# A hybrid attention layer on one core: z of the softmax heads made before v, gate sigmoids moved, half of P divided by ScalarE

## The chip, the cores and the metric

The kernel runs on one core of one Trainium2 chip. The time is device microseconds (us) of one launch. Engines: PE (TensorE), PEld (its weight loads), DVE (VectorE), ACT (ScalarE), POOL (GpSimd) and SP (SyncE, which here only issues DMAs). Each engine works through its own queue in order.

## The reference, cut to what matters

x is 512 x 1024, one batch, one layer; eight softmax heads (branch a) and eight stick-breaking heads (branch b), each 64 wide.

```python
h = rms_norm(x, norm_w)
qa, ka, va, za, qb, kb, vb, zb, gl_a, gl_b = split(h @ w_in)     # 8 x 512, 2 x 1024
oa = moba_attention(rms_norm(qa), rms_norm(ka), va, rel_bias)    # softmax(q k / 8 + bias[t - s]), s <= t
ob = stick_breaking_attention(qb, kb, vb)                        # A[t,s] = b_ts * prod_{s<j<t}(1 - b_tj)
ya = (oa * silu(za)) @ w_up_moba
yb = (ob * silu(zb)) @ w_up_sb
y  = sigmoid(gl_a + gb[:1024]) * ya + sigmoid(gl_b + gb[1024:]) * yb
return x + y @ w_out
```

## The kernel before

**Products in three parts.** Every fp32 operand is split into a high and a low half in fp32r, and each product is three matmuls (mm3, L233 high by low, L234 low by high, L235 high by high). For a weight block the low half is therefore read by the second matmul of its chunk.

**Weights.** They come as blocks of 128 x 1024 (512 KB, `wr`), loaded by SP (L159) in a fixed order, split by ACT into `wh` (L187) and by DVE into `wl` (L189). Each of the three has 3 buffers, so wl of block n+3 can be made only when block n has been used up. The number in a tile's name (wl55) is the block's place in that order. A chunk of one block is 24 matmuls over 512 columns.

**Stages.** First qa and ka with their row norms; then the seven chunks of FRONT while the norms and the transposed q and k are made; then v (values, blocks of sums and differences in seven products X, Y, Z) and q of branch b; then eight pairs of heads, a0 to a3 and b0 to b3; at the end the up products of b and the output projection.

**A pair of heads.** PE makes the scores of two heads (L512), then the weighted sum with v of the pair two before (weighted, L604; its result `po` is multiplied by z at L609 and split at L750 and L751). Per head of a, softmax() (L526) loads the bias, adds it and takes the row's extreme (DVE L532), takes Exp with the row sum (ACT L534), the reciprocal (DVE L535) and divides the rows (DVE L537). Rows come as four tiles, tile 3 with 512 columns to tile 0 with 128. Per head of b, stick() (L542) takes two sigmoids of each tile (ACT L550, L551, L560, L561), a scan of running products (DVE L554, L564) and a multiply (DVE L556, L566). Then P is transposed in 32 x 32 blocks (turn, DVE L576), written to memory by four SP DMAs (put, L583) and read back by a DMA of ACT's queue (get, L590).

**The fills.** Between these steps PE gets chunks from the table FILLS, four entries a pair: one behind P of each head, and two after that. The words are za and zb (f_z: sigmoid of the chunk on ACT L617, multiplied by it on DVE L618, both read the PSUM bank), k and q (split(), ACT L420 and DVE L421), g (f_g: a gate chunk, evicted by one ACT Sigmoid with the bias, L631), and up (the up product of a, multiplied into the gates at L769). Chunks that stand in the front use the six PSUM banks of tag "s"; in the pairs those of tag "pj", which has two.

**What sets the order.** The list scheduler of the framework puts the instructions of each engine into its queue by data dependences and its own estimates; `issue_after` adds a dependence where the code wants one (in stick(), for example, the first sigmoid of a pair comes after the last weight split, and the sigmoids of the second head after the last gate eviction in `evicted`). Exp and Sigmoid lie in different tables of ACT, so each change between them has an ACT_TABLE_LOAD in the queue.

Of the kernel before, what the change touches and what calls it, by code (L numbers as in the profile page):

```python
# [12 lines left out]
AF = mybir.ActivationFunctionType  # L13
ALU = mybir.AluOpType
# [28 lines left out]
Y_SUMS = {0: ("T2b",), 2: ("T3a", "T3b"), 5: ("T4a", "T4b")}  # L43


FRONT = ("g:0", "g:1", "g:2", "g:3", "g:4", "g:5", "g:6")
FILLS = ("za:0", "k:0 q:0", "", "",
         "za:1", "g:7 q:1", "k:1", "",
         "za:2", "g:8", "zb:0", "",
         "za:3", "k:2 q:2", "g:9", "",  # L50
         "zb:1", "g:10", "k:3 q:3", "",
         "zb:2", "g:11", "up:0", "",
         "zb:3", "g:12", "up:1", "",
         "g:13", "g:14", "up:2", "up:3",
         "g:15")


@with_exitstack
def hybrid_layer(ctx: ExitStack, tc: tile.TileContext, x, xT, w, rel, out):
    nc = tc.nc  # L60
    V, A, G, T = nc.vector, nc.scalar, nc.gpsimd, nc.tensor
# [16 lines left out]
    def slot(name, dt=F32):  # L78
        return gp.tile([P, S], dt, tag="g", name=name)
# [15 lines left out]
    nw, mb, qw, kw = sm[:, 0:8], sm[:, 8:24], sm[:, 24:25], sm[:, 25:26]  # L95
# [8 lines left out]
    VOUT, QOUT = ([(kind, b + h) for b in ORDER[kind] for h in HALVES[kind]] for kind in "vq")  # L104
    stream = list(range(8)) + list(range(20, 20 + len(FRONT))) + VOUT + QOUT + list(range(20 + len(FRONT), WO)) + OUT

# [24 lines left out]
    def each(step, kind, names, after):  # L131

        for name in names:
            for half in HALVES[kind]:
                after = step(kind, name, half, after)
        return after
# [224 lines left out]
    def mix_x(k):  # L361

        a, b = xraw[k], xraw[k + 4]
        left, right = slice(0, HS), slice(HS, S)
        V.tensor_tensor(b[:, right], a[:, right], b[:, right], op=ALU.subtract)
        V.tensor_tensor(a[:, right], a[:, left], a[:, right], op=ALU.subtract)
        V.tensor_tensor(a[:, left], b[:, right], a[:, left], op=ALU.subtract)
        V.tensor_tensor(b[:, left], b[:, left], a[:, left], op=ALU.add)
        h = tp.tile([P, 4 * PQ], F32R, tag="pt", bufs=4, name=f"mx{k}")
        if k < 2:  # L370
            l = tp.tile([P, 4 * PQ], F32R, tag="turned", bufs=2, name=f"ml{k}")
            l = [l[:, n * S:(n + 1) * S] for n in range(2)]
        else:
            l = [tp.tile([P, S], F32R, tag=("p3", "sx")[n], bufs=2, name=f"ml{k}{n}") for n in range(2)]
        for n, raw in enumerate((a, b)):
            hi, lo = h[:, n * S:(n + 1) * S], l[n]
            A.activation(hi, raw, AF.Copy)
            V.tensor_tensor(lo, raw, hi.bitcast(F32), op=ALU.subtract)
            for cs, name in ((left, ("S2", "S4")[n]), (right, ("S3", "S1")[n])):
                mixed[name, k] = hi[:, cs], lo[:, cs]  # L380
# [68 lines left out]
    def split_flipped(raws, name):  # L449

        res = []
        for p, raw in enumerate(raws):
            hi, lo = slot(f"{name}{p}h", F32R), slot(f"{name}{p}l", F32R)
            src = raw.rearrange("p (a i r) -> p i a r", a=4, i=NT)
            h, l = (by_block(blocks(x)) for x in (hi, lo))
            if name == "qa":
                whole = slot(f"{name}{p}")
                A.activation(by_block(mirror(whole)), src, AF.Copy, scale=nqk)
                src, h, l = whole, hi, lo
            A.activation(h, src, AF.Copy)  # L460
            V.tensor_tensor(l, src, h.bitcast(F32), op=ALU.subtract)
            res.append((hi, lo))
        return res
# [5 lines left out]
    def norm(ps, name, **order):  # L469
        st[name] = head_norm(ps, name, **order)  # L470

    def spread(ps, name):
        with tc.issue_after(low[count[0] - 2]):
            rows = head_rows(ps, name, st[name])
        flipped[name] = flip(rows, name)
# [3 lines left out]
    def bring(name):  # L479
        raws[name] = fetch(flipped[name], name)  # L480
# [11 lines left out]
    def chunk_ct(name):  # L492
        hi, lo = load_w()
        ps = bank(home[0], name)
        for k in range(KT):
            ks = slice(k * P, (k + 1) * P)
            mm3(ps, hi[:, ks], lo[:, ks], xH[k], xL[k], k == 0, k == KT - 1)
        return ps
# [20 lines left out]
    def row_tiles(br, h):  # L519

        p10 = tp.tile([P, 3 * P], F32, tag="p1", bufs=2, name=f"p{br}{h}1")
        return {3: tp.tile([P, S], F32, tag="p3", bufs=2, name=f"p{br}{h}3"),
                2: tp.tile([P, 3 * P], F32, tag="p2", bufs=2, name=f"p{br}{h}2"),
                1: p10[:, :2 * P], 0: p10[:, 2 * P:], (1, 0): p10}

    def softmax(h, sc, bias):  # L526
        rows = row_tiles("a", h)
        m = tp.tile([P, 3, NT], F32, tag="m", bufs=4, name=f"m{h}")
        for two in ((3, 2), (1, 0)):
            for i in two:  # L530
                n = (i + 1) * P
                V.tensor_tensor_reduce(rows[i], sc[i], bias[:, S - n:], scale=1.0, scalar=3e38, op0=ALU.add,  # L532
                                       op1=ALU.min, accum_out=m[:, 0, i:i + 1])
                A.activation(rows[i], rows[i], AF.Exp, bias=m[:, 0, i:i + 1], scale=-1.0, accum_out=m[:, 1, i:i + 1])  # L534
            V.reciprocal(m[:, 2, two[1]:two[0] + 1], m[:, 1, two[1]:two[0] + 1])  # L535
            for i in two:
                V.tensor_scalar(rows[i], rows[i], m[:, 2, i:i + 1], None, op0=ALU.mult)  # L537
        return rows

    evicted = []  # L540
# [73 lines left out]
    def f_z(br, p):  # L614
        ps = chunk_ct(f"z{br}{p}")
        zr[br, p] = slot(f"z{br}{p}")
        A.activation(zr[br, p], ps, AF.Sigmoid)  # L617
        V.tensor_tensor(zr[br, p], ps, zr[br, p], op=ALU.mult)  # L618
# [7 lines left out]
    gates = {}  # L626

    def f_g(i):
        ps = chunk_ct(f"gl{i}")
        g = slot(f"gl{i}")  # L630
        evicted.append(A.activation(g, ps, AF.Sigmoid, bias=mb[:, i:i + 1]).ins)  # L631
        gates[i] = g

    for i, word in enumerate(FRONT):
        f_g(int(word.split(":")[1]))
        if i == 0:
            norm(ps_ka, "ka", after=summed[0])
            mix_x(0)
        elif i == 1:
            mix_x(1)  # L640
            summed.append(each(add_sum, "v", ("T3",), last["ka"]))
        elif i == 2:
            bring("qa")
            mix_x(2)
        elif i == 3:
            spread(ps_ka, "ka")
            mix_x(3)
        elif i == 4:
            bring("ka")
        elif i == 5:  # L650
            qa.extend(split_flipped(raws["qa"], "qa"))
# [152 lines left out]
    def split_3(k):  # L804
# [2 lines left out]
        part(*s3[k], gates[k], slice(0, HS))  # L807


    make = {"za": lambda i: f_z("a", i), "zb": lambda i: f_z("b", i), "q": f_q, "k": f_k, "g": f_g,  # L810
            "up": lambda i: up("a", i)}
    fills = [[(kind, int(i)) for kind, i in (word.split(":") for word in part.split())] for part in FILLS]

    def fill(tag="pj"):

        for kind, i in fills.pop(0):
            home[0] = "s" if kind == "up" else tag
            make[kind](i)
# [7 lines left out]
    def finish(m, tag="s"):  # L826

        br, p = PAIRS[m]
        weighted(tag, br, p, v_of[br], [done.pop((m, b)) for b in range(2)])
        split_o(br, p)  # L830

    early[0] = True
    for m, (br, p) in enumerate(PAIRS):
        q, k = (qa, ka) if br == "a" else (qb, kb)
        sc = {h: {} for h in (2 * p, 2 * p + 1)}
        with tc.issue_after(end[0]):
            scores(br, p, q, k, sc)
        if m > 1:
            finish(m - 2, "pj")
        for b in range(2):  # L840
            h = 2 * p + b
            bias = load_bias(h) if br == "a" else None
            done[m, b] = put(br, h, turn(br, h, (softmax if br == "a" else stick)(h, sc[h], bias)))
            fill()
            if not b:
                done[m, 0] = get(*head(m, 0), done[m, 0])
        for b in range(2):
            if not b:
                done[m, 1] = get(*head(m, 1), done[m, 1])
            if (m, b) in SUMS:  # L850
                sum_w(SUMS[m, b], done[m, b])
            fill("pj" if (b or not fills[1]) and m < 7 else "s")
# [77 lines left out]
    for c in range(2):  # L930
        hi, lo = load_w()
        for t, ps, a, b in parts:
            for kk in range(2):
                k = 2 * c + kk
# [20 lines left out]
def _layout(x, norm_w, w_in, merge_gate_b, q_norm_w, k_norm_w, rel_bias, w_up_moba, w_up_sb, w_out):  # L955
# [24 lines left out]
    first = {"za": 1536, "g": 4096, "k": 2560, "zb": 3584}  # L980
    for kind, i in (word.split(":") for word in " ".join(FRONT + FILLS).split()):
        if kind == "up":
# [32 lines left out]
```

## Time and profile before

| what | value |
|---|---|
| median of three runs (lowest, highest) | 384.65 us (384.2, 386.11) |
| profiled execution | 384.15 us |
| span of its instructions | 382.4 us |
| mean granted clock of PE | 0.999 |
| HBM read and written | 67.65 MB and 14.70 MB |

The profile is one execution. A row of a group shows its busy time, the mean of one in ns, and the idle time before it with what ended it. A row of the timeline begins with its start and its length in us; matmul lengths overlap, so their rate is read from their starts. L numbers are lines of the kernel before; those of the kernel after are up to 12 higher.

### The profile page before, as it was taken

What the parts mean: (1) busy time and instruction counts of PE and PEld (TensorE: products, weight loads), DVE (VectorE), ACT (ScalarE), POOL (GpSimd) and SP (SyncE); (2) the same over time, 40 slices, a digit from 0 to 9 for tenths busy, and PEclk for the clock granted to TensorE, in tenths of its full rate; (3) what the DMA queues carried; (4) which work ended last, traced back from release to release, by engine and by line L of the source; (5) the groups of instructions that cost most, each with busy time, mean ns of one, the idle gap of its engine ahead of it and who ended that gap; (6) DMA issues with size and microseconds to landing.
All of it is one profiled execution on the core that took longest, in us unless ns stands there. A gap on an engine that the chain in (4) does not pass through costs nothing.

```text
span 382.4 us, 5493 instructions
## 1 busy us (share of the span) xinstructions
PE 377.9 (99%) x1935; PEld 308.8 (81%) x1935; DVE 290.9 (76%) x503; ACT 211.3 (55%) x353; POOL 78.5 (21%) x124
## 2 busy tenths in 40 slices
PE   8999999999999999999999999999999999999996
PEld 5888888888888998887887878787878877888885
DVE  4828998934786468993889689798988825999962
ACT  5675657346754537772886773553554322368540
POOL 3859959220210200000000000010000000420310
PEclk9999999999999999999999999999999999999999
DMA  7989898996673755869767765869788881599964
GB/s 271 340 328 340 212 198 301 252 326 245 152 197 92 204 128 183 210 207 285 244 162 236 224 235 154 285 165 312 248 242 285 207 301 56 157 264 292 163 164 172
DMA packets 36747, 86.38 MB, mean 226 GB/s; under 512 B 3944, under 2 KB 16744, under 8 KB 36720
## 3 DMA queue, kind: packets, MB, share of 16 engines
q1 hardware_dynamic: 27696, 52.72, 41.2%
q0 software_dynamic: 6576, 22.57, 25.0%
q10 hardware_dynamic: 2448, 10.75, 8.5%
q8 instruction: 15, 0.25, 0.3%
q14 instruction: 12, 0.10, 0.1%
HBM read 67.65 MB, written 14.70 MB: 215 GB/s over the span
## 4 chain that ended last, share of the span: by engine, by line
PE 99%; DVE 0%; issue 0%
PE gl L233 8%; PE gl L234 8%; PE gl L235 8%; PE poa L604 2%; PE pob L604 2%; PE sb L512 2%; PE sa L512 2%; PE za L233 2%; PE zb L233 2%; PE yb L233 2%; PE za L234 2%; PE zb L234 2%; PE yb L234 2%; PE ka L234 2%; PE ka L233 2%; PE kb L234 2%
## 5 line engine op out<-in xcount | busy, mean ns | idle before, releaser
L189 DVE TENSOR_TENSOR wl<-wr,wh 128x1024 fp32r<-128x1024 f32 (+1 forms) x61 | 71.8, 1181 | 31.6 <-ACT wh L187 31.5
L187 ACT ACTIVATE wh<-wr 128x1024 fp32r<-128x1024 f32 (+1 forms) x61 | 62.8, 1029 | 41.0 <-DMA wr<-in_w 9.6
L233 PE MATMUL gl<-xl,wh 128*128 128x512 f32 x128 | 50.0, 390 | 0.0
L234 PE MATMUL gl<-xh,wl 128*128 128x512 f32 x128 | 49.9, 390 | 0.0
L235 PE MATMUL gl<-xh,wh 128*128 128x512 f32 x128 | 49.8, 389 | 0.0
L140 POOL COPY turn_of<-ptb 1x1 f32<-1x1 f32 x3 | 0.7, 245 | 147.9 <-DMA ptb<-pdb 147.9
L233 PEld LDWEIGHTS gl<-xl,wh 128*128 128x128 f32 x128 | 24.0, 188 | 5.3 <-issue 0.2
L235 PEld LDWEIGHTS gl<-xh,wh 128*128 128x128 f32 x128 | 24.0, 188 | 5.0
L234 PEld LDWEIGHTS gl<-xh,wl 128*128 128x128 f32 x128 | 24.0, 188 | 4.9
L631 ACT ACTIVATE gl<-gl,x 128x512 f32<-128x512 f32 x16 | 11.0, 686 | 23.1 <-PE gl L235 22.7
L554 DVE TENSOR_TENSOR_SCAN sx<-om,begin 128x512 f32<-128x512 f32 (+1 forms) x16 | 17.0, 1078 | 4.5 <-ACT om L550 4.5
L534 ACT ACTIVATE pa<-pa,m 128x512 f32<-128x512 f32 (+3 forms) x32 | 17.6, 552 | 1.4 <-DVE m L532 1.3
L576 DVE STREAM_TRANSPOSE turnedb<-pb 128x384 f32<-128x384 f32 (+1 forms) x24 | 14.0, 602 | 0.1
L532 DVE CUSTOM_DVE_ANT_0 pa<-sa,om 128x512 f32<-128x512 f32 (+3 forms) x32 | 13.9, 485 | 0.0
L576 DVE STREAM_TRANSPOSE turneda<-pa 128x384 f32<-128x384 f32 (+1 forms) x24 | 13.7, 602 | 0.0
L233 PE MATMUL za<-xl,wh 128*128 128x512 f32 x32 | 12.9, 404 | 0.0
L233 PE MATMUL zb<-xl,wh 128*128 128x512 f32 x32 | 12.8, 400 | 0.0
L233 PE MATMUL yb<-olb,wh 128*128 128x512 f32 x32 | 12.6, 393 | 0.0
L234 PE MATMUL za<-xh,wl 128*128 128x512 f32 x32 | 12.5, 390 | 0.0
L234 PE MATMUL zb<-xh,wl 128*128 128x512 f32 x32 | 12.5, 390 | 0.0
L234 PE MATMUL yb<-ohb,wl 128*128 128x512 f32 x32 | 12.5, 390 | 0.0
L234 PE MATMUL ka<-wh,xl 128*128 128x512 f32 x32 | 12.5, 390 | 0.0
(428 smaller groups left out, 1070.6 us busy)
## 6 DMA issues: line engine op xcount, KB each, us to landing
wr<-in_w SPq DMA_DIRECT2D x57, 512.0 KB, 5.6
pda<-turneda SPq DMA_DIRECT2D x32, 160.0 KB, 2.9
pta<-pda ACTq DMA_DIRECT2D x8, 640.0 KB, 4.5
pdb<-turnedb SPq DMA_DIRECT2D x32, 160.0 KB, 4.2
ptb<-pdb ACTq DMA_DIRECT2D x8, 640.0 KB, 6.3
qT<-in_w POOLq DMA_DIRECT2D x6, 512.0 KB, 6.3
xn<-in_x SPq DMA_DIRECT2D x8, 256.0 KB, 6.5
om<-e_dr SPq DMA_DIRECT2D x8, 256.0 KB, 4.1
```

The lines of the kernel that those rows point to most:

```text
L187: high[c] = A.activation(hi[:, a:b], raw[:, a:b], AF.Copy).ins
L189: low[c] = V.tensor_tensor(lo[:, a:b], raw[:, a:b], hi[:, a:b].bitcast(F32), op=ALU.subtract).ins
L233: T.matmul(ps, aH, bL, start=start, stop=False, skip_group_check=on)
L234: T.matmul(ps, aL, bH, start=False, stop=False, skip_group_check=on)
L235: end[0] = T.matmul(ps, aH, bH, start=False, stop=stop, skip_group_check=on).ins
L512: T.matmul(ps[b][:, c:c + n], x[o, i * P:(i + 1) * P], y[o, :n], start=m == 0, stop=m == 2)
L532: V.tensor_tensor_reduce(rows[i], sc[i], bias[:, S - n:], scale=1.0, scalar=3e38, op0=ALU.add, op1=ALU.min, accum_out=m[:, 0, i:i + 1])
L534: A.activation(rows[i], rows[i], AF.Exp, bias=m[:, 0, i:i + 1], scale=-1.0, accum_out=m[:, 1, i:i + 1])
L554: V.tensor_tensor_scan(sx[:, n - 1::-1] if n == S else sx[:, :n][:, ::-1], om[:, S + 1 - n:][:, ::-1], begin[:, S - n:S][:, ::-1], 0.0, op ...
L576: V.transpose(turned[:, :, at:at + n, :].rearrange("p q j r -> p j q r"), rows[i].rearrange("p (j q c) -> p j q c", j=n, q=4))
L604: guard[0] = T.matmul(po[o, :].rearrange("p (a n r) -> p a n r", a=4, r=32)[:, :, i:i + n, :], vv[j][:, c:c + HD], src, start=j == NT - 1, ...
L631: evicted.append(A.activation(g, ps, AF.Sigmoid, bias=mb[:, i:i + 1]).ins)
```

## The change

It has four parts. FRONT holds three gates and the four z chunks of branch a in place of seven gates. FILLS is written anew: gates g:3 to g:10 stand beside the softmax pairs, z of b beside its own pairs, in each pair's first entry. A gate chunk made in a softmax pair is evicted with Identity plus bias and gets its Sigmoid later, in place, from a new word "s" in the entries of pairs b0, b1 and b2, behind the newest gate eviction. In softmax() the divides of tiles 3 and 2 go from DVE to ACT (Copy with a scale per row); tiles 1 and 0 stay.

```diff
-FRONT = ("g:0", "g:1", "g:2", "g:3", "g:4", "g:5", "g:6")
+FRONT = ("g:0", "g:1", "g:2", "za:0", "za:1", "za:2", "za:3")
...
-         "za:3", "k:2 q:2", "g:9", "",
-         "zb:1", "g:10", "k:3 q:3", "",
+         "k:2 q:2", "g:9", "g:10", "",
+         "zb:0", "g:11", "k:3 q:3 s:3 s:4", "",
...
             for i in two:
-                V.tensor_scalar(rows[i], rows[i], m[:, 2, i:i + 1], None, op0=ALU.mult)
+                if i > 1:
+                    A.activation(rows[i], rows[i], AF.Copy, scale=m[:, 2, i:i + 1])
+                else:
+                    V.tensor_scalar(rows[i], rows[i], m[:, 2, i:i + 1], None, op0=ALU.mult)
...
-        evicted.append(A.activation(g, ps, AF.Sigmoid, bias=mb[:, i:i + 1]).ins)
+        evicted.append(A.activation(g, ps, AF.Identity if raw[0] else AF.Sigmoid, bias=mb[:, i:i + 1]).ins)
...
+    raw = [False]
+
+    def f_s(i):
+        with tc.issue_after(evicted[-1]):
+            A.activation(gates[i], gates[i], AF.Sigmoid)
+
     for i, word in enumerate(FRONT):
-        f_g(int(word.split(":")[1]))
+        kind, n = word.split(":")
+        f_g(int(n)) if kind == "g" else f_z("a", int(n))
...
     for m, (br, p) in enumerate(PAIRS):
+        raw[0] = br == "a"
```

The table moves instructions on all engines. Three places follow; the number behind an underscore only tells tiles of one name apart.

**Place 1, ACT's queue at the end of pair a3, before.** `pa7` are the rows of head 7 with their Exp, `m7` its row numbers, `pta6` the read of head 6's transposed rows, `wh48` a weight split, `om1` the first sigmoid of pair b0.

```order
L534 ACTIVATE pa73_2164,m7_2166<-pa73_2164,m7_2166 128x512
L534 ACTIVATE pa72_2165,m7_2166<-pa72_2165,m7_2166 128x384
L534 ACTIVATE pa71_2163,m7_2166<-pa71_2163,m7_2166 128x256
L534 ACTIVATE pa71_2163,m7_2166<-pa71_2163,m7_2166 128x128
L187 ACTIVATE wh47_2190<-wr47_2130 128x1024
L420 ACTIVATE kb2h_2221<-kb2_2196 128x512
L590 DMA pta6_2160<-pda6_2121 128x1280
L420 ACTIVATE qb2h_2225<-qb1_1260 128x512
L187 ACTIVATE wh48_2231<-wr48_2194 128x1024
L631 ACT_TABLE_LOAD
L631 ACTIVATE gl9_2262<-gl9_2237,x0_78 128x512
L550 ACTIVATE om1_121<-sb03_2264 128x512
```

The same place in the changed kernel:

```order
L594 DMA pta6_2165<-pda6_2121 128x1280
L188 ACTIVATE wh47_2195<-wr47_2130 128x1024
L635 ACTIVATE gl10_2261<-gl10_2236,x0_78 128x512
L535 ACTIVATE pa73_2169,m7_2171<-pa73_2169,m7_2171 128x512
L535 ACTIVATE pa72_2170,m7_2171<-pa72_2170,m7_2171 128x384
L535 ACTIVATE pa71_2168,m7_2171<-pa71_2168,m7_2171 128x256
L535 ACTIVATE pa71_2168,m7_2171<-pa71_2168,m7_2171 128x128
L539 ACTIVATE pa73_2169<-pa73_2169,m7_2171 128x512
L539 ACTIVATE pa72_2170<-pa72_2170,m7_2171 128x384
L188 ACTIVATE wh48_2230<-wr48_2199 128x1024
L554 ACT_TABLE_LOAD
L554 ACTIVATE om1_121<-sb03_2263 128x512
```

The eviction of the pair's last gate (gl9 before, gl10 now), which stood behind the Exps of head 7, now stands ahead of them, and gl9's ahead of that; behind them are the two divides, the weight split and the one table load before om1.

**Place 2, DVE's queue at the start of pair b1, before.** `wl` are weight splits, `sx2` and `pb2` scans and rows of head 2 of branch b, `oa3` and `ola3` the last output of branch a.

```order
L189 TENSOR_TENSOR wl50_2402<-wr50_2342,wh50_2401 128x1024
L189 TENSOR_TENSOR wl51_2437<-wr51_2405,wh51_2436 128x1024
L421 SCALAR_TENSOR_TENSOR kb3l_2468<-kb3_2442,kb3h_2467 128x512
L554 SCALAR_TENSOR_TENSOR sx23_2531<-om1_121,begin_108 128x512
L556 TENSOR_TENSOR pb23_2527<-pb23_2527,sx23_2531 128x512
L554 SCALAR_TENSOR_TENSOR sx22_2536<-om0_120,begin_108 128x384
```

The same place in the changed kernel:

```order
L190 TENSOR_TENSOR wl50_2401<-wr50_2341,wh50_2400 128x1024
L422 SCALAR_TENSOR_TENSOR kb3l_2467<-kb3_2441,kb3h_2466 128x512
L422 SCALAR_TENSOR_TENSOR qb3l_2471<-qb1_1264,qb3h_2470 128x512
L613 TENSOR_TENSOR oa3_2521<-poa3_2510,za3_970 128x4x128
L762 TENSOR_TENSOR ola3_2524<-oa3_2521,oha3_2523 128x512
L190 TENSOR_TENSOR wl51_2436<-wr51_2404,wh51_2435 128x1024
L558 SCALAR_TENSOR_TENSOR sx23_2532<-om1_121,begin_108 128x512
L558 SCALAR_TENSOR_TENSOR sx22_2537<-om0_120,begin_108 128x384
```

The first scan of the pair came after kb3l; now it comes after oa3, ola3 and wl51. In SP's queue the load of block 51, which stood ahead of the eight writes of pair b0, now stands behind them.

**Place 3, DVE's queue in pair b2, before.** `sx4`, `pb4` and `turnedb4` belong to the pair's first head, those with a 5 to the second; `ob0` and `olb0` are the output of pair b0; wl55 is the block of up:1.

```order
L564 SCALAR_TENSOR_TENSOR sx41_2751<-om_short_116,begin_108 128x386
L609 TENSOR_TENSOR ob0_2730<-pob0_2719,zb0_2048 128x512
L566 TENSOR_TENSOR pb41_2736<-pb41_2736,sx41_2751 128x384
L189 TENSOR_TENSOR wl55_2764<-wr55_2655,wh55_2763 128x1024
L751 TENSOR_TENSOR olb0_2733<-ob0_2730,ohb0_2732 128x512
L576 STREAM_TRANSPOSE turnedb4_2754<-pb41_2736 128x3x4x32
L554 SCALAR_TENSOR_TENSOR sx53_2804<-om1_121,begin_108 128x512
```

The same split in the changed kernel:

```order
L570 TENSOR_TENSOR pb51_2803<-pb51_2803,sx51_2818 128x384
L580 STREAM_TRANSPOSE turnedb5_2821<-pb53_2804 128x4x4x32
L580 STREAM_TRANSPOSE turnedb5_2821<-pb52_2805 128x3x4x32
L580 STREAM_TRANSPOSE turnedb5_2821<-pb51_2803 128x3x4x32
L190 TENSOR_TENSOR wl55_2768<-wr55_2656,wh55_2767 128x1024
L622 TENSOR_TENSOR zb2_2798<-zb2_2773,zb2_2798 128x512
```

wl55 moved from the middle of the first head to behind the last transpose of the second.

More of the change, by code (lines that the diff above doesn't have):

```diff
@@ L43 @@
 Y_SUMS = {0: ("T2b",), 2: ("T3a", "T3b"), 5: ("T4a", "T4b")}
-FRONT = ("g:0", "g:1", "g:2", "g:3", "g:4", "g:5", "g:6")
-FILLS = ("za:0", "k:0 q:0", "", "",
-         "za:1", "g:7 q:1", "k:1", "",
-         "za:2", "g:8", "zb:0", "",
-         "za:3", "k:2 q:2", "g:9", "",
-         "zb:1", "g:10", "k:3 q:3", "",
-         "zb:2", "g:11", "up:0", "",
-         "zb:3", "g:12", "up:1", "",
-         "g:13", "g:14", "up:2", "up:3",
+FRONT = ("g:0", "g:1", "g:2", "za:0", "za:1", "za:2", "za:3")
+FILLS = ("k:0 q:0", "g:3", "", "",
+         "g:4 q:1", "g:5", "k:1", "",
+         "g:6", "g:7", "g:8", "",
+         "k:2 q:2", "g:9", "g:10", "",
+         "zb:0", "g:11", "k:3 q:3 s:3 s:4", "",
+         "zb:1", "g:12", "up:0 s:5 s:6 s:7", "",
+         "zb:2", "g:13", "up:1 s:8 s:9 s:10", "",
+         "zb:3", "g:14", "up:2", "up:3",
          "g:15")
@@ L807, in split_3 @@
         part(*s3[k], gates[k], slice(0, HS))
-    make = {"za": lambda i: f_z("a", i), "zb": lambda i: f_z("b", i), "q": f_q, "k": f_k, "g": f_g,
+    make = {"za": lambda i: f_z("a", i), "zb": lambda i: f_z("b", i), "q": f_q, "k": f_k, "g": f_g, "s": f_s,
             "up": lambda i: up("a", i)}
```

## The prediction

> **What bounds the kernel.** I read the page's busy times and chain first, then what PE waited for, then the stretches of the stick-breaking pairs.
>
> ```profile
> PE 377.9 (99%) x1935; PEld 308.8 (81%) x1935; DVE 290.9 (76%) x503; ACT 211.3 (55%) x353; POOL 78.5 (21%) x124
> PE 99%; DVE 0%; issue 0%
> PE pwarm L223 <- DVE warm L87: 1.0, 1, 1.0
> ```
>
> PE is busy for 99% of the span, the chain that ended last is PE itself, and the waits of PE hold one row, 1.0 us at the start. Nothing that lightens ACT or DVE can shorten this; it can only lengthen when PE has to wait. So the sum below asks at every place when what PE needs is ready, and when PE gets there. The slack is thinnest in the pairs b0, b1, b2 (us, then PE, PEld, DVE, ACT, POOL, the granted clock, the DMA share and GB/s):
>
> ```profile
> 219.40:240.40 21.00, 21.00 (x119) 16.60 (x118) 17.14 (x24) 10.75 (x19) 0.00 (x0) 1.00 0.64 202
> 240.40:261.30 20.90, 20.90 (x117) 16.50 (x116) 19.04 (x27) 10.41 (x19) 1.81 (x3) 1.00 0.73 222
> 261.30:282.20 20.90, 20.90 (x117) 16.59 (x116) 18.53 (x26) 10.56 (x19) 1.58 (x3) 1.00 0.79 256
> ```
>
> DVE has 21.0 - 17.1 = 3.9, 1.9 and 2.4 us idle per pair: work that comes late can be caught up by that much only.
>
> **What goes and what is added, off the path.** Groups by form (busy us, mean ns, idle before):
>
> ```profile
> L534 ACT ACT_TABLE_LOAD x6 | 7.7, 1283 | 0.1
> L537 DVE TENSOR_SCALAR pa<-pa,m 128x512 f32<-128x512 f32 x8 | 3.9, 487 | 0.2
> L537 DVE TENSOR_SCALAR pa<-pa,m 128x384 f32<-128x384 f32 x8 | 3.3, 415 | 0.0
> L617 ACT ACTIVATE za<-za 128x512 f32<-128x512 f32 x4 | 2.4, 599 | 2.1 <-PE za L235 2.1
> L618 DVE TENSOR_TENSOR za<-za,za 128x512 f32<-128x512 f32 x4 | 2.7, 664 | 0.3 <-ACT za L617 0.3
> L550 ACT ACTIVATE om<-sb 128x384 f32<-128x384 f32 x8 | 4.0, 497 | 0.0
> ```
>
> ACT loses ten of its 14 table loads, 10 x 1.28 = 12.8 us, and gets 16 divides (no row shows one; as ACT's nearest forms, 8 x 0.60 + 8 x 0.50 = 8.8) and eight gate sigmoids of their own (8 x 0.60 = 4.8): +0.8. DVE loses 3.9 + 3.3 = 7.2 us of divides. PE waits for neither engine, so all of this is worth 0; the cover is PE's own 5.44 us chunks (24 matmuls, one every 0.227 us). A gain is excluded, since no PE wait but the first 1.0 us is there to go.
>
> The front: four z chunks take the place of g:3 to g:6, and each holds its bank until its multiply on DVE, 0.66 after the sigmoid.
>
> ```profile
> 49.64 0.23 PE gl L233
> 100.87 0.69 DVE L461 TENSOR_TENSOR qa3l<-qa,qa3h 128x512 fp32r<-128x512 f32 x1
> 182.12 0.69 DVE L609 TENSOR_TENSOR oa<-poa,za 128x512 f32<-128x512 f32 x1 [3.07 <-PE poa L604]
> ```
>
> The last, za3's, now stands behind qa3l, so its bank is free at about 100.87 + 0.6 + 0.7 = 102.2. The bank that it keeps is wanted by product Z, ten chunks after the front's start: 49.64 + 10 x 5.44 = 104.0. It fits by 1.8, and one more weight split (1.15) ahead of it on DVE would still fit: 0. z is first read at 182.12, so it is never late.
>
> **The end of pair a3 (place 1).** Of before:
>
> ```profile
> 210.60 0.72 ACT L534 ACTIVATE pa<-pa,m 128x512 f32<-128x512 f32 x1
> 212.80 1.05 ACT L187 ACTIVATE wh<-wr 128x1024 fp32r<-128x1024 f32 x1
> 219.57 0.69 ACT L631 ACTIVATE gl<-gl,x 128x512 f32<-128x512 f32 x1 [2.02 <-PE gl L235]
> 220.46 0.60 ACT L550 ACTIVATE om<-sb 128x512 f32<-128x512 f32 x1 [0.21 <-PE sb L512]
> 221.09 1.22 DVE L554 TENSOR_TENSOR_SCAN sx<-om,begin 128x512 f32<-128x512 f32 x1 [2.43 <-ACT om L550]
> ```
>
> The Exps of head 7 ran from 210.60 to 212.80. In the changed order ACT has the evictions of gl9 and gl10 ahead of them. gl10's chunk is the last of a3, where gl9's was, so its eviction also starts near 219.57 and is done near 220.15. Then stand 2.2 us of Exp (222.35), two divides of 0.60 + 0.50 (223.45), wh48 1.0 (224.4), the one table load 1.28 (225.7) and om: the first scan of b0 starts at about 226.3, where it was 221.09. DVE is 5.2 us late. PE is not:
>
> ```profile
> 240.45 2.07 PE sb L512 x24
> 314.14 4.47 PE pob L604 x40
> ```
>
> wl48 is for the second chunk of b0, after the scores (2.07 from 219.4), one product (half of 4.47) and a chunk of 5.44, at 229.1; wh48 at 224.4 and 1.15 of DVE make it by 226.
>
> **Pairs b0 and b1 (place 2).** One stick head costs DVE six us, from the first scan to the last transpose of one head that ran alone:
>
> ```profile
> 284.61 2.07 DVE L554 TENSOR_TENSOR_SCAN sx<-om,begin 128x512 f32<-128x512 f32 x2
> 290.64 0.65 DVE L609 TENSOR_TENSOR ob<-pob,zb 128x512 f32<-128x512 f32 x1
> 269.33 1.22 DVE L189 TENSOR_TENSOR wl<-wr,wh 128x1024 fp32r<-128x1024 f32 x1
> 278.03 2.32 DVE L189 TENSOR_TENSOR wl<-wr,wh 128x1024 fp32r<-128x1024 f32 x2
> 236.12 2.12 SPq L583 DMA_DIRECT2D pdb<-turnedb  x4
> wr<-in_w SPq DMA_DIRECT2D x57, 512.0 KB, 5.6
> 250.57 0.40 PE L234 MATMUL gl<-xh,wl 128*128 128x512 f32 x1
> 256.04 0.39 PE L234 MATMUL ya<-oha,wl 128*128 128x512 f32 x1
> ```
>
> 290.64 - 284.61 = 6.03 per head; a weight split is 1.15 (2.32 for two), other DVE work of 512 columns 0.6. From 226.3: two heads 12.0, ola2 0.6, wl49 1.15, zb0 0.6: the second head is transposed at 240.65. On SP the load of wr51 is now queued behind all eight transposed writes of b0; the last four of them take 2.1 (242.8), the block lands 5.6 later (248.4), wh51 takes 1.0 on ACT (249.4), wl51 1.15 (250.6). PE wants it at 250.57: wait 0. Ends: if the split is done as soon as ACT is free it is ready 2 us earlier, and a landing of 8 makes it 2.4 late. I take the median landing.
>
> The order has wl51 ahead of b1's scans, so these start at 250.6; one head 6.0 and wl52 1.15 end at 257.75. PE wants wl52 at 256.04, in the second matmul of the pair's third chunk. **Wait 1.7.**
>
> **Pair b2 (place 3).** Before, wl55 stood in the middle of the first head of b2 (269.33); now it stands behind the second.
>
> ```profile
> 276.96 0.39 PE L234 MATMUL ya<-oha,wl 128*128 128x512 f32 x1
> ```
>
> From 257.75 on DVE: zb1 0.6, b1's second head 6.0, wl53 and wl54 2.3, two gate products 1.2 (267.85); b2's first head 6.0 with ob0 and olb0 1.2 (275.05); second head 6.0 (281.05); wl55 1.15: 282.2. PE wants it at 276.96, moved by the wait so far to 278.66. **Wait 3.55**, 5.25 in all.
>
> **Pair b3 and the last heads.**
>
> ```profile
> 286.71 0.43 PE gl L233
> 303.10 0.39 PE L233 MATMUL ya<-ola,wh 128*128 128x512 f32 x1
> 299.85 4.43 SPq L583 DMA_DIRECT2D pdb<-turnedb  x4
> 307.11 0.33 ACTq L590 DMA_DIRECT2D ptb<-pdb  x1
> ptb<-pdb ACTq DMA_DIRECT2D x8, 640.0 KB, 6.3
> ```
>
> pob1 ends where the chunk at 286.71 starts: with the waits, 292.0. ob1 0.6, wl57 1.15, olb1 0.6 (294.35), head 6.0, wl58 1.15 (301.5, not late), zb3 0.6, head 6.0 (308.1), wl59 1.15: 309.25. PE wants wl59 at 303.10 + 5.25 + 0.68 (three matmuls on) = 309.0: **wait 0.25.** The last head's write to memory starts at 308.1 where it was 299.85. Its read was issued 307.11 - 299.85 = 7.26 after that, so at 315.4, and lands 6.3 later at 321.7. PE wants it at 314.14 + 5.5, plus the first half of the two products' 4.47 = 2.24: 321.9. With 8.0 for the landing the wait would be 1.5; I take **0.5**.
>
> **The sum** is made on the profiled execution, 384.15 us (span 382.4 and 1.75 around it), which is 0.5 below the median of 384.65. 384.15 + 1.7 + 3.55 + 0.25 + 0.5 = 390.15, so 390.2, slower by 1.4 to 1.6%. A measurement of this kernel tells some 0.5%, 1.9 us, from no change.
>
> **Rivals.**
>
> *DVE catches up: no change.* The same mechanism, but the lag of 5.2 us is worked off before wl55. For it: the idle 3.9 + 1.9 us of b0 and b1, and the 7.2 us relieved on DVE. Against: the divides were relieved in the a pairs, before the lag arises, and the idle time was counted in above. It decides when DVE reaches wl55's split 3.4 to 4.1 us sooner than in the sum: the first two waits together are then 1.2 to 1.9. Even with no lag at all, two heads, ob0 and olb0 and the split from b2's first scan (262.98 of before) give 262.98 + 13.2 + 1.15 = 277.3 against 276.96, 0.4 late:
>
> ```profile
> 262.98 1.23 DVE L554 TENSOR_TENSOR_SCAN sx<-om,begin 128x512 f32<-128x512 f32 x1 [0.83 <-ACT om L550]
> ```
>
> So 0.4 to 1.9 us: about 385.0, from 384.6 to 386.0. Chance 0.22.
>
> *Half of it.* wr51 lands early and wl51 is made 2.2 us sooner; then wl52 is in time and wl55 waits 5.25 - 2.2 = 3.05; with none to all of the last 0.75 it comes to 387.2 to 387.95, about 387.6. Chance 0.11.
>
> *A slow clock after the wait.* The first nine matmuls after idling took 4.0 / 9 = 0.447 us each, where the steady ones start every 0.227:
>
> ```profile
> L223 PE MATMUL pwarm<-warm 128*128 128x512 bf16 x9 | 4.0, 631 | 1.0 <-DVE warm L87 1.0
> 0.98:5.00 4.02, 4.02 (x10) 1.42 (x10) 0.71 (x2) 2.32 (x4) 2.49 (x10) 1.00 0.69 218
> ```
>
> If PE runs at that pace for about 3.5 us after the wait of 3.55 at wl55, it loses 3.5 x (1 - 0.227/0.447) = 1.7 more: 391.9, and with the last read late by 1.5, 393. The Trainium skill's page "TensorE: Matmul & The Clock Gate", section "Part 1: The HAM clock gate", says that the array's clock is halved after about one idle window (~3.4 us) and is whole again after as long of sustained work; by that rule a wait of 3.55 would just be enough. The opening matmuls agree with a halved rate, though the granted clock of the profile reads 1.00 there too; no wait in the middle of this trace shows whether it comes back. It decides when the wait at wl55 stays in one piece. Chance 0.10.
>
> *Faster* by over 0.5% would need PE's own work to shrink; the matmuls are the same. Chance 0.02.
>
> **The numbers.** The sum above has 0.55 (own bounds 388.6 to 392.6: without the last two waits and 0.8 less at wl55, or with the landing of 8 at wr51, which makes all behind it 2.4 later), the catch-up 0.22, half of it 0.11, the slow clock 0.10, faster 0.02. Slower: 0.55 + 0.11 + 0.10 = 0.76; same 0.22; faster 0.02. The range goes from 384.9, which leaves out the lower part of the catch-up case (0.1) and faster (0.02), to 393.0 (0.05 left out above).
>
> **What would show it.** In the profile of after: the waits of PE with rows for wl (L190) near 256, 278 and 309 of the old time, the middle one longest; ACT's Exp of head 7 after 220; the first scan of b0 near 226; wl55's split last before PE's wait, with the transposes of the second b2 head ahead of it; four table loads. Wrong would be: PE still at one wait row (then the queue orders cost less than the rows say), a wait in the front or at v (za3's bank), or PE waiting for ACT's wh with DVE idle.

## The result and the profile after

The changed kernel takes 388.32 us (median of five runs, 388.02 to 388.56) against 384.2: a ratio of 1.0096 (95% interval 1.0072 to 1.012), slower by about 1%. A ratio is taken from the fast runs, in which the kernel before itself spreads from 383.8 to 389.6 us over all experiments, so it can differ a little from that of the medians and can lie just under 1 without a gain. The profiled execution took 388.29 us with a span of 386.5, 4.1 us more than before. The forecast was 390.2 with a range of 384.9 to 393.0: the sign and the kind of wait were right, the sum was 1.9 us too large, and one of its causes was put in the wrong place.

The page of the changed kernel: busy time, then the engines' shares of the chain that ended last, then the waits of PE.

```profile
PE 379.2 (98%) x1935; PEld 308.3 (80%) x1935; DVE 284.5 (74%) x487; ACT 211.2 (55%) x367; POOL 80.0 (21%) x124
PE 82%; DVE 6%; DMA 5%; ACT 3%; issue 2%; SPq 2%; DVEq 0%
PE ya L235 <- DVE wl L190: 1.8, 2, 1.3
PE pwarm L224 <- DVE warm L88: 1.0, 1, 1.0
PE sb L513 <- ACT pb L555: 0.6, 1, 0.6
PE qa L282 <- ACT wh L188: 0.3, 1, 0.3
```

ACT is as busy as before and DVE has 6.4 us less to do, and neither helped. The chain, which was PE alone, now leaves PE: it runs through DVE, ACT and DMAs for almost a fifth of the span. PE waits twice for a weight split in an up product (`ya`) and once in the scores (`sb`).

Where the time came from is read by laying PE's starts side by side. The scores of b0 begin at 219.20 (219.46 before, so the front and the softmax pairs lost nothing), those of b1 at 240.19 (240.38), and the up products of b at 322.68 (318.54). From the first of these points to the last it was 99.08 us and is 103.48: all of the loss, 4.4 us, lies in the stick-breaking pairs, less 0.26 gained ahead of them. It has three places: 0.80 in the first up product (b1), 1.67 in the scores of b2, 1.68 in the second up product (b2); 0.25 is spread over b3. The idle times in the rows are shorter than these losses, since the lengths of matmuls overlap.

The timeline of the changed kernel at the end of pair a3 and the start of b0 (start, length; the bracket is the idle time before and what ended it):

```profile
216.61 0.69 DVE L533 CUSTOM_DVE_ANT_0 pa<-sa,om 128x512 f32<-128x512 f32 x1 [6.26 <-DMA om<-e_dr]
219.31 0.69 ACT L635 ACTIVATE gl<-gl,x 128x512 f32<-128x512 f32 x1 [3.10 <-PE gl L236]
219.90 0.71 ACT L535 ACTIVATE pa<-pa,m 128x512 f32<-128x512 f32 x1
225.55 0.60 ACT L554 ACTIVATE om<-sb 128x512 f32<-128x512 f32 x1
226.18 2.07 DVE L558 TENSOR_TENSOR_SCAN sx<-om,begin 128x512 f32<-128x512 f32 x2
```

The Exp of head 7 waits behind gate 10, as the order said, and the first scan of b0 starts at 226.18 (226.3 in the sum). The first row shows something that the order of ACT and DVE could not: head 7's bias rows came only at 216.6. Their load was requested at 209.7, behind the writes of an earlier head, where before it was requested at 198.7, ahead of them.

The turn from b0 to b1, of before (SP's loads and writes, DVE's first scan):

```profile
217.70 3.13 SPq L159 DMA_DIRECT2D wr<-in_w  x3
228.52 9.73 SPq L583 DMA_DIRECT2D pdb<-turnedb  x8
238.34 3.17 SPq L159 DMA_DIRECT2D wr<-in_w  x3
242.06 1.23 DVE L554 TENSOR_TENSOR_SCAN sx<-om,begin 128x512 f32<-128x512 f32 x1 [0.25 <-ACT om L550]
```

and of the changed kernel (SP, ACT, DVE):

```profile
232.80 10.14 SPq L587 DMA_DIRECT2D pdb<-turnedb  x8
243.04 6.96 SPq L160 DMA_DIRECT2D wr<-in_w  x4
247.32 1.06 ACT L188 ACTIVATE wh<-wr 128x1024 fp32r<-128x1024 f32 x1 [1.28 <-DMA wr<-in_w]
248.42 1.23 DVE L190 TENSOR_TENSOR wl<-wr,wh 128x1024 fp32r<-128x1024 f32 x1 [1.64 <-ACT wh L188]
249.56 2.06 DVE L558 TENSOR_TENSOR_SCAN sx<-om,begin 128x512 f32<-128x512 f32 x2
```

Behind the writes there are three block loads before and four now, and block 51 is the first of the four. It is requested at 243.0, when the eight writes are out. ACT is idle for 1.28 us until it lands, and DVE for 1.64 us until ACT has split it. b1's scans, which the code orders behind that block's split, begin 7.5 us later than before. The three waits that follow on PE, with the two DVE operations that end them:

```profile
256.70 0.50 PE L235 MATMUL ya<-oha,wl 128*128 128x512 f32 x1 [0.51 <-DVE wl L190]
264.05 0.38 PE L513 MATMUL sb<-kb2l,qb2h 64*128 64x256 f32 x1 [0.64 <-ACT pb L555]
265.30 1.28 DVE L780 TENSOR_TENSOR gl<-ya,gl 128x512 f32<-128x512 f32 x2
279.47 1.18 DVE L190 TENSOR_TENSOR wl<-wr,wh 128x1024 fp32r<-128x1024 f32 x1
280.71 0.50 PE L235 MATMUL ya<-oha,wl 128*128 128x512 f32 x1 [1.34 <-DVE wl L190]
```

The second was not in the sum. The two results of the up product (ya0, ya1) hold two of the six "s" banks until DVE multiplies them at 265.30 (259.83 and 261.45 before), so the last scores of b2 have to wait for banks of the same pair's first tiles, until ACT has read them. The matmuls of the two heads, which start in pairs before, then start one by one; that is why 1.67 us are lost where the row shows an idle time of 0.64.

### The profile page after: what moved, and what is told of

It is laid out like the page before. It is cut to its first block, busy times and chain, and to the rows that moved or that the text cites. A ratio compares the mean times of both kernels' runs of the same rounds, so it can differ in the third digit from the quotient of the medians.

```text
span 386.5 us, 5481 instructions
## 1 busy us (share of the span) xinstructions
PE 379.2 (98%) x1935; PEld 308.3 (80%) x1935; DVE 284.5 (74%) x487; ACT 211.2 (55%) x367; POOL 80.0 (21%) x124
## 4 chain that ended last, share of the span: by engine, by line
PE 82%; DVE 6%; DMA 5%; ACT 3%; issue 2%; SPq 2%; DVEq 0%
PE gl L234 6%; PE gl L235 6%; PE gl L236 6%; DMA pdb<-turnedb 3%; PE sa L513 2%; DMA wr<-in_w 2%; PE yb L234 2%; PE yb L235 2%; PE ka L235 2%; PE ka L234 2%; PE vx L235 2%; PE vx L234 2%; PE za L235 2%; PE za L234 2%; PE ka L236 2%; PE yb L236 2%
## 5 line engine op out<-in xcount | busy, mean ns | idle before, releaser
L141 POOL COPY turn_of<-ptb 1x1 f32<-1x1 f32 x3 | 2.3, 758 | 148.9 <-DMA ptb<-pdb 148.9
L235 PE MATMUL ya<-oha,wl 128*128 128x512 f32 x32 | 12.8, 401 | 1.8 <-DVE wl L190 1.8
L234 PE MATMUL kb<-xl,wh 128*128 128x512 f32 x32 | 12.7, 398 | 0.0
L236 PE MATMUL ya<-oha,wh 128*128 128x512 f32 x32 | 12.5, 390 | 0.0
```

The source lines that it names most:

```text
L141: with tc.issue_after(G.tensor_copy(turn_of, done[:1, :1].bitcast(F32)).ins):
L234: T.matmul(ps, aH, bL, start=start, stop=False, skip_group_check=on)
L235: T.matmul(ps, aL, bH, start=False, stop=False, skip_group_check=on)
L236: end[0] = T.matmul(ps, aH, bH, start=False, stop=stop, skip_group_check=on).ins
```

## The experiments

Each kernel is compared with the kernel before on the same chip. The first eight were laid out for the theory of the prediction: a lag of DVE at the start of b0 is what costs.

**Gate 10 behind the Exps of head 7** (f_g, and the last Exp noted in softmax()):

```diff
+        with tc.issue_after(exps[7]) if i == 10 else nullcontext():
             evicted.append(A.activation(g, ps, AF.Identity if raw[0] else AF.Sigmoid, ...
```

> The eviction of gate 10 put behind the Exps of head 7 on ACT; all else as changed. Theory (DVE enters pair b0 late, and queue places turn that into waits of PE): the Exps start when the bias sum is there, near 217.3 instead of 219.9, so the first scan of b0 comes near 224.3 instead of 226.2; the waits of PE in b1 and b2 shrink to 1 to 2 us in all: 385.2 to 386.3 us. Rival (the new table of fills costs in the stick-breaking pairs by itself, without the lag): 387.5 to 388.5. Rival (the divides on ACT): 388.3.

Measured: 394.25 us, 1.0223 (1.0173 to 1.0272). The first scan of b0 came at 224.57 and that of b1 at 242.04, as in the kernel before, so the lag was gone there. But with the dependence the scheduler laid the queues out anew, and now the load of block 54 stands behind the eight writes of b1: only two loads, 52 and 53, come between the writes of b0 and those of b1. Of that run, SP, then ACT and DVE in b2:

```profile
240.76 1.80 SPq L160 DMA_DIRECT2D wr<-in_w  x2
249.86 11.71 SPq L587 DMA_DIRECT2D pdb<-turnedb  x8
261.67 8.95 SPq L160 DMA_DIRECT2D wr<-in_w  x4
267.95 1.06 ACT L188 ACTIVATE wh<-wr 128x1024 fp32r<-128x1024 f32 x1 [2.99 <-DMA wr<-in_w]
270.79 2.07 DVE L558 TENSOR_TENSOR_SCAN sx<-om,begin 128x512 f32<-128x512 f32 x2
```

b2's first scan is at 270.79 (262.98 before). The same picture as in the changed kernel, one pair later, without the lag in front of it. Theory and rivals all had the wrong number here.

**The bias rows through POOL's queue** (load_bias):

```diff
-        nc.sync.dma_start(bt, bass.AP(tensor=e_dr.tensor, ...
+        nc.gpsimd.dma_start(bt, bass.AP(tensor=e_dr.tensor, ...
```

> The bias rows of the softmax heads loaded by POOL's queue instead of SP's, where head 7's stood behind eight transposed writes and a weight block and landed at 216.4; all else as changed. Theory: the Exps of head 7 then run before gates 9 and 10 are evicted, the first scan of b0 is back at 221 to 222, and PE's waits in b1 and b2 go: 383.9 to 384.9 us, no difference from the kernel before. Rival (table of fills by itself): 387 to 388.5. Rival (divides on ACT): 388.3.

Measured: 386.17 us, 1.0025 (0.9995 to 1.0056), above the theory's range and below the rivals'. No wait of PE is left in the stick-breaking pairs, but one came in the front, where the first two loads now stand ahead of the row norms on POOL:

```profile
PE psR L349 <- ACT diag L345: 1.6, 1, 1.6
```

**A weight split ahead of the second head** (stick()):

```diff
-            with tc.issue_after(split_of[1]) if h % 2 == 0 and i == 3 else nullcontext():
+            with tc.issue_after(split_of[1]) if i == 3 else nullcontext():
```

> As changed, but the first scan of each second stick-breaking head stands behind the newest weight split, which puts the split of block 55 between the two heads of b2 instead of behind both; the lag at the start of b0 stays. Theory: the wait of 1.7 at block 55 goes, those before it (0.8 at block 52 and 1.7 in the scores of b2) stay: 386.4 to 386.9 us. Rival (what waits there is held up by something else than the place of the split): 388.0 to 388.5.

Measured: 387.51 us, 1.0036 (1.0002 to 1.0071); the profiled execution 386.46. The wait at block 55 is gone, the one in the scores of b2 has stayed at 1.66, and the one at block 52 shrank to 0.3, with no row of its own:

```profile
PE sb L513 <- ACT pb L555: 0.6, 1, 0.6
```

From the scores of b0 to the up products of b it is 101.14, 2.06 above before, where the first two waits of the changed kernel were 2.47. So in the profiled execution the place of that split was worth its share and 0.5 us at block 52 besides. The median lies 0.6 above the theory's range; its longer runs have no profile, so what they lost stays open.

**All divides on DVE again** (softmax(), `if i > 1` made `if i > 3`):

> As changed, but all four tiles of P are divided by DVE again. Theory: at the end of a3 ACT is 1.2 us sooner and DVE 0.9 later, so the lag of 5.2 shrinks by about 0.3 to 1 and the time is 387.2 to 388.2 us. Rival (the divides on ACT are what costs): 384.0 to 385.0.

Measured: 388.44 us, 1.0083 (1.0054 to 1.0112), 0.2 above the theory's range. The divides on ACT are not the cause.

**The bias rows on POOL from the third head on** (`(nc.gpsimd if h > 1 else nc.sync).dma_start`):

> As the run with the bias rows on POOL's queue, but the first two heads' rows stay on SP, so that they no longer stand ahead of the row norms on POOL. Theory (the wait of 1.6 at the spread of the norms there came from those two loads, and the waits in the stick-breaking pairs are gone with the lag): no wait of PE beyond 1.0 but at the start, 383.9 to 384.9 us. Rival (the wait at the spread has another cause): 385.5 to 386.5.

Measured: 384.64 us, 0.9974 (0.9942 to 1.0005). All the waits of PE in it:

```profile
PE pwarm L224 <- DVE warm L88: 1.0, 1, 1.0
```

Everything of the change is in this kernel, and it costs nothing; nor does it gain.

**The kernel before with more work for DVE in b0** (stick()):

```diff
+            for _ in range(10 if h == 0 and i == 3 else 0):
+                V.tensor_scalar(sx, om[:, :S], 1.0, None, op0=ALU.mult)
```

> The kernel before with ten idle multiplies of 512 columns on DVE (10 x 0.49 = 4.9 us) ahead of the first scan of b0; nothing else added, the result unchanged. Theory that the lag alone costs: waits of PE in b1 and b2 as in the changed kernel, 386.5 to 388.5 us. Rival (the lag is worked off in the idle 3.9 + 1.9 us unless the loads and splits also stand late in their queues): 384.0 to 385.3.

Measured: 384.41 us, 0.9984 (0.9964 to 1.0004). DVE was late indeed: the writes of b0 ended on SP at 242.9 (238.2 before; 242.9 in the changed kernel too). But block 51 had been requested ahead of them, and b1 began 1.7 us later than before only:

```profile
236.30 6.62 SPq L585 DMA_DIRECT2D pdb<-turnedb  x8
243.78 2.07 DVE L556 TENSOR_TENSOR_SCAN sx<-om,begin 128x512 f32<-128x512 f32 x2
```

That speaks against the theory: the lag by itself cost nothing. It isn't quite alone here, though, since the scheduler also put two more loads, 52 and 53, ahead of the writes. The run with block 51 on POOL's queue, below, has the lag with these loads behind the writes.

**Only the front** (z of branch a there, gates 3 to 6 where z was):

```diff
-FRONT = ("g:0", "g:1", "g:2", "g:3", "g:4", "g:5", "g:6")
-FILLS = ("za:0", "k:0 q:0", "", "",
+FRONT = ("g:0", "g:1", "g:2", "za:0", "za:1", "za:2", "za:3")
+FILLS = ("g:3", "k:0 q:0", "", "",
```

> The kernel before with only the front changed: za:0 to za:3 in place of g:3 to g:6 there, and these four gates where z was; gates evicted with Sigmoid in place, all divides on DVE. Theory (za3's bank is free 1.8 us before product Z wants it; nothing else changes): 383.9 to 384.9 us. Rival (the multiply of za3 on DVE comes late and v waits for its bank): 385 to 387.

Measured: 384.2 us, 0.9971 (0.9944 to 0.9997), with a span of 382.5 (382.4 before). v did not wait.

**Gates with Sigmoid at once** (the changed kernel without `raw[0] = br == "a"` and without the words "s"):

> As changed, but every gate is evicted with Sigmoid at once and the eight later sigmoids are left out (14 table loads again). Theory (the lag comes from the queues at the end of a3, not from the later sigmoids): the order puts head 7's Exps ahead of gates 9 and 10 here, so the first scan of b0 comes nearer to 221 and the time lies at 384.0 to 386.0 us. Rival (table of fills and place of block loads alone): 387 to 388.5.

Measured: 390.63 us, 1.0141 (1.0099 to 1.0183), above the ranges of theory and rival. Of this run, DVE's first scan of b0, then ACT and DVE at the start of b1:

```profile
221.12 1.23 DVE L558 TENSOR_TENSOR_SCAN sx<-om,begin 128x512 f32<-128x512 f32 x1 [2.42 <-ACT om L554]
245.03 1.06 ACT L188 ACTIVATE wh<-wr 128x1024 fp32r<-128x1024 f32 x1 [3.42 <-DMA wr<-in_w]
248.46 2.06 DVE L558 TENSOR_TENSOR_SCAN sx<-om,begin 128x512 f32<-128x512 f32 x2
```

No lag at all in b0, and still b1 begins 6.4 us late, behind a block that lands late. Here too block 51 is queued behind the eight writes.

So the theory was changed: what decides is where SP's queue has the block load that the next pair's first scan stands behind, ahead of the eight writes of the pair or behind them. The last runs turn that one thing around in both kernels.

**The changed kernel with block 51 through POOL's queue** (load_w):

```diff
-            nc.sync.dma_start(begun[c], w[stream[c]])
+            (nc.gpsimd if c == 51 else nc.sync).dma_start(begun[c], w[stream[c]])
```

> As changed, but the load of weight block 51 goes through POOL's queue, so that it no longer stands behind the eight writes of pair b0 on SP. The Exps of head 7 still stand behind gate 10, and the first scan of b0 still comes near 226. Theory now (the late block load in front of pair b1 is what turns the lag into waits, since the pair's first sigmoid and scan stand behind that block's split): b1's first scan comes near 244 instead of 249.6, no wait of PE in b1 and b2 over 0.5, 384.0 to 385.3 us. Rival (the lag at the start of b0 alone): 387 to 388.5.

Measured: 384.46 us, 0.9962 (0.9932 to 0.9992). The lag is there, as large as in the changed kernel, and is worked off: b0's first scan comes 6.98 us after its first scores in both, where it was 1.63 before. Of the waits in the b pairs none is left (the one of 0.5 lies in q, before the pairs). The profiled execution, 385.45, is the longest of its runs, and PE came to b0's scores 1.1 us later than in the kernel before:

```profile
227.57 2.07 DVE L558 TENSOR_TENSOR_SCAN sx<-om,begin 128x512 f32<-128x512 f32 x2
244.52 2.06 DVE L558 TENSOR_TENSOR_SCAN sx<-om,begin 128x512 f32<-128x512 f32 x2
PE pwarm L224 <- DVE warm L88: 1.0, 1, 1.0
PE qe L235 <- DVE wl L190: 0.5, 1, 0.5
```

**The kernel before with block 51 behind the eight writes** (load_w; put() notes its last write):

```diff
-            nc.sync.dma_start(begun[c], w[stream[c]])
+            with tc.issue_after(putted[0]) if c == 51 else nullcontext():
+                nc.sync.dma_start(begun[c], w[stream[c]])
```

> The kernel before with only one thing changed: the load of block 51 is ordered behind the eight writes of pair b0 on SP. No lag in b0. Theory: the block lands near 243.9, b1's first scan comes near 246.3 instead of 242.1, which is 4 us of lag with some slack left: 384.2 to 386.5 us, waits if any in b2. Rival (the place of the load is enough by itself): 387 to 391.

Measured: 389.69 us, 1.0095 (1.0057 to 1.0132). Nothing of the change is in it, and its ratio is that of the changed kernel. The waits lie in the scores of b2, as there, and in an up product of b3, and some 1.7 us of the loss in the profiled execution are a slower clock after the second of them (last section). In three runs of it the mean granted clock was 1.00, and these took 388.9 to 389.0 us, so without the slower clock the load's place still costs some 4 us. SP, DVE, and the waits of PE:

```profile
228.88 9.79 SPq L584 DMA_DIRECT2D pdb<-turnedb  x8
238.77 8.87 SPq L160 DMA_DIRECT2D wr<-in_w  x4
246.06 1.22 DVE L190 TENSOR_TENSOR wl<-wr,wh 128x1024 fp32r<-128x1024 f32 x1
247.80 2.06 DVE L555 TENSOR_TENSOR_SCAN sx<-om,begin 128x512 f32<-128x512 f32 x2
PE ya L235 <- DVE wl L190: 1.8, 1, 1.8
PE sb L513 <- DVE gl L770: 1.3, 2, 1.1
```

The second wait names the banks: the scores wait for the multiply that frees ya. This was the rival's number; I had given the load's place too little.

**Both in the kernel before** (the ten multiplies and the late block):

> The kernel before with both: the ten idle multiplies of DVE in b0 and the load of block 51 behind the eight writes. Theory (lag and late load together make the waits): 386.5 to 390 us, though nothing of the change is in it. Rival (something else of the change is needed): 384.0 to 385.5.

Measured: 392.96 us, 1.0191 (1.0132 to 1.0249), above the theory's range. Nothing else of the change is needed; the lag adds its part once the load stands behind the writes (b1's first scan at 253.38). About half of what it loses beyond the run with the late block alone is a second stretch of slow clock.

**Only the divides** (softmax() of the changed kernel in the kernel before):

> The kernel before with only the divides of tiles 3 and 2 on ACT. Theory (ACT and DVE have room in the softmax pairs): 383.9 to 385.0 us. Rival (each divide on ACT delays the transposes and with them the writes): 385.5 to 388.

Measured: 385.45 us, 0.999 (0.9956 to 1.0024), between the two ranges and no difference clear of the noise. The profiled execution has one new wait of PE, in pair a1, for a bank that z's multiply holds; so this part isn't quite free where z is made in the pairs:

```profile
PE kb L233 <- DVE za L621: 1.2, 1, 1.2
```

Taken together (the change of the time from b0's scores to the up products of b against 99.08 us before, from the profiles):

| kernel | block load behind the eight writes | first scan of b0, b1, b2 | PE lost there |
|---|---|---|---|
| before | none | 221.1, 242.1, 263.0 | 0 |
| bias rows on POOL from head 2 on | none | 222.4, 242.2, 263.1 | 0 |
| bias rows all on POOL | none | 224.0, 243.8, 264.7 | 0 |
| front only | none | 221.2, 242.2, 263.1 | 0 |
| before, divides only | none | 222.3, 243.3, 264.1 | 0 |
| before, more work in b0 | none | 232.6, 243.8, 262.9 | 0 |
| changed, block 51 on POOL | none | 227.6, 244.5, 264.1 | 0 |
| changed | 51 | 226.2, 249.6, 266.5 | 4.4 |
| changed, divides on DVE | 51 | 225.8, 249.4, 266.3 | 3.8 |
| changed, split ahead of the second head | 51 | 226.4, 249.4, 266.3 | 2.1 |
| changed, Sigmoid at once | 51 | 221.1, 248.5, 266.0 | 6.8 |
| before, block 51 late | 51 | 221.5, 247.8, 264.7 | 5.8 |
| before, both | 51 | 232.7, 253.4, 269.7 | 9.0 |
| changed, gate 10 behind Exp | 54 | 224.6, 242.0, 270.8 | 8.9 |

(First scan: the first one over 512 columns; where b0 has more work, the scheduler put this one later in the head and others ahead of it.) In the runs with all bias rows on POOL, with the divides only and with block 51 on POOL, PE itself comes to b0's scores 1.1 to 1.8 later than before, and the scans with it.

Every kernel with a late block lost time in these pairs, and none without one did, whatever the lag. The losses above 5 us hold stretches of slow clock as well, an estimated 1.7 us each from the granted clock of the stretches: one in "gate 10 behind Exp", "Sigmoid at once" and "block 51 late", two in "both". Without them these four lost 4.1 to 7.2.

## Why the prediction was right, and where it was not

- *Nothing to gain.* Right: PE had no wait to lose, and the best of the kernels that hold all of the change (384.46 and 384.64) stand where the kernel before stands (384.2). The first has a ratio just under 1 (0.9962); its shortest run is 384.1, that of the kernel before next to it 383.9.
- *What goes and what is added is worth 0.* Right for the changed kernel (ACT 211.3 to 211.2 us busy; the run with the divides back on DVE is no faster). ACT has four table loads left, as forecast. The divides by themselves cost 1.2 in the old order in the profiled execution, which the ratio of that run (0.999) can't tell from nothing.
- *The front fits by 1.8 us.* Right: the run with the front alone does not wait.
- *Place 1, the first scan of b0 at 226.3.* Right as a number (226.18). It was not ACT's order alone, since head 7's bias rows came late too; and, against the prediction, this lag decides nothing by itself: 4.7 us of it in the kernel before (the end of b0's writes) cost 0, and so did the whole 5.35 us of it (from b0's first scores to its first scan) in the changed one with the block moved.
- *Place 2, wl51 at 250.6.* It was made at 249.6. The sum has the late load in it, so its number held. But the prediction took the lag for the cause and the place of the load for a part of its path; the runs show the reverse. This is the step that was wrong: by itself the load behind the writes brings b1's first scan to 247.8, the lag by itself to 243.8. It shows most in the catch-up rival, which had only 0.4 us lost with no lag at all; the kernel before with block 51 late has no lag in b0 and lost 5.8.
- *Wait 1.7 at wl52.* Measured 0.80; DVE finished it at 256.65 instead of 257.75.
- *No term for the scores of b2.* Measured 1.67. The banks of tag "s" were not followed in the sum, though the up product takes two of them until DVE gets to its multiplies.
- *Wait 3.55 at wl55.* Measured 1.68. The split was ready at 280.6 instead of 282.2, and PE came 0.6 later than in the sum, having waited in the scores. With the two waits before, the loss up to here is 4.15 where the sum had 5.25.
- *0.25 in b3, 0.5 at the last read.* The first is right as a number (0.25), but the profile has no row of a wait at wl59, and the loss is spread over the pair; the last read came in time.
- *The total.* It is near in part by luck: the sum had 0.9 too much at wl52, 1.87 at wl55 and 0.5 at the last read, and the 1.67 in the scores that it left out made up for half of that.
- *The rivals.* DVE's catching up did happen within the b pairs, but not far enough. The clock stayed at 1.00 in the changed kernel; a slower one is met in other runs, below.

## What to carry to other kernels

When one queue carries both early loads and late stores, the order in that queue can matter more than any engine's load (here some 4 us for the place of one block, against 0 for a lag of DVE): a load that stands behind stores inherits the lateness of the work which makes them, and everything ordered behind the load stands still with it. Before blaming a late start, look what lies ahead of the next stage's input in its DMA queue, and test the place of that one transfer; and follow the banks that a late engine keeps, not only its results.

## What the runs showed of the hardware

The clock. In the kernel before with block 51 late, PE waited 1.83 us in one piece, at 300.4. PE's first matmul after it, and the stretches before, after and then (the granted clock is the third number from the end):

```profile
302.22 0.50 PE L235 MATMUL ya<-oha,wl 128*128 128x512 f32 x1 [1.83 <-DVE wl L190]
296.00:300.00 4.00, 4.00 (x20) 3.30 (x18) 4.00 (x7) 4.00 (x9) 1.11 (x2) 1.00 0.65 231
302.20:306.00 3.80, 3.78 (x10) 3.05 (x11) 3.80 (x6) 0.59 (x1) 0.00 (x0) 0.58 1.00 186
306.00:310.00 4.00, 4.00 (x18) 3.22 (x18) 4.00 (x7) 0.00 (x0) 0.00 (x0) 0.98 0.79 167
```

For 3.8 us the mean granted clock was 0.58. From 302.22 on ten matmuls took 3.96 us, most of them 0.41 to 0.43 apart, where ten take 2.27 at 0.227; so 1.7 us were lost on top of the wait, of the 5.8 in the table. In other runs the waits of 2.40 us (gate 10 behind the Exps), 2.22 (Sigmoid at once) and 1.78 (both in the kernel before) were followed by 3.8 us at 0.69, 0.66 and 0.71, and so were two close together, 1.66 and 0.76, in the last of these (0.71). The changed kernel's longest wait, 1.34, left the clock at 1.00. Waits of 1.47 (gate 10 behind the Exps) and 1.59 (bias rows on POOL) left it there as well. The Trainium skill's page "TensorE: Matmul & The Clock Gate", section "Part 1: The HAM clock gate", gives about 3.4 us of idling for the drop and as long again for the return; the return agrees here, the drop came after about half of that. For this kernel the measured waits count, not the page's figure for the drop.
